# The last chunk of w_down: earlier sums copied into the banks ahead of the products

## The chip, the core and the metric

The kernel runs on one core of a Trainium2 chip. The metric is device time in microseconds (us), the median of several runs. A core has five engines that work through their own instruction queues and wait for each other by semaphores: PE (matrix products into eight PSUM banks of 128 x 512 fp32), ACT and DVE (elementwise work; both reach SBUF and PSUM), POOL and SP (here used to issue DMAs; POOL's can add into their destination, SP's can't).

## The reference

One encoder layer on 512 tokens of width 2048, all in fp32: RMSNorm, one input projection, dilated attention beside gated linear attention, output projection, residual. Then the part that matters here:

```python
h = rmsnorm(x, ffn_norm_w[l])
x = x + (jax.nn.silu(h @ w_gate[l]) * (h @ w_up[l])) @ w_down[l]
return rmsnorm(x, final_norm_w)
```

The hidden width is 5632, so w_down is 5632 x 2048.

## The kernel before

**fp32 from three products.** Every operand is split into a rounded part hi and a rest lo; a product is hi·hi + hi·lo + lo·hi, three matmuls. ACT makes hi by a copy that rounds, DVE makes lo by a subtraction. In `Down.products` the three are L2022 (needs hi), L2023 (needs lo of w_down) and L2024.

**w_down in seven products.** The class `Down` computes most of `g @ w_down` by a Strassen-like scheme with seven products in place of eight, M0 to M6 (`n` in the code, in the order of `ORDER`: 0, 6, 1, 3, 4, 2, 5). The rows of w_down that it covers are cut into four chunks of eight 128-row tiles, the columns into two halves C of 1024. `run` walks through `seq`: chunk, then C, then the seven products k, then two depths d. One entry is a **step** of 12 matmuls. A product is two steps long and fills two banks. A half is 14 steps; the code calls the steps of the last half of the last chunk l = 0 to 13, and those of the half before it are l = -14 to -1.

**A step's own work.** `cast(i+2)` on ACT (L1991) and `sub(i+2)` on DVE (L1999) make hi and lo for the step after next. From the fourth product on the operand is a sum of blocks, made one step earlier by `add(i+3)` on DVE (L1976, L1979). `evac_late` copies the two banks of the product that has just ended to SBUF (ACT, L2062 for n = 4, which changes the sign, L2064 for the others).

**What happens to a product's sum.** Its copy goes to `md` in DRAM: written by SP in the first chunk (L2069), added to what is there by an accumulating DMA from POOL in the others (L2067). After the last chunk each of the 14 sums (two halves of seven) must be read back: `fetch` (L2045, a DMA on POOL's queue, 512 KB). For the half C = 0 this stands at l = 1 to 7, for C = 1 at l = 5 to 13 and after the loop. The very last product (C = 1, n = 5) is not added in DRAM; DVE adds its banks to the fetched sum (L2057).

**Combining.** `combine(C)` turns the seven sums into four outputs in seven entries of two DVE additions each (L2084). `step(C, n)` does the next n entries; for C = 0 they stand at l = 5 to 11, for C = 1 in the first job after `run` (1, 0, 3, 3 entries in its four parts). `seed` (L2101, ACT) copies four results into banks, on which a later job then accumulates.

**What follows.** Four jobs `later_jobs`, one for each 512 columns, add 4 more row tiles of w_down onto the seeded banks; each has four parts of 12 matmuls (L346, L347, L348). Their w_down pieces come through the stream `st`: SP loads 512 KB (L209), ACT rounds a half piece (L237), DVE takes the rest (L218). `g_load` and `g_split` (L1816, L1824 to L1828) do the same for the tiles of g. At the end of a job `residual` (L1847, DVE, four times) adds the banks to x; `seed(c+1)` stands in the job's third part. Then `finish` does the last four row tiles and the final norm.

**What sets the order.** The order in each queue is that of the program text, written out by hand. SBUF buffers come from two pools of slots, first in first out: `s4` (33 slots of 4 KB per partition) and `s2`. An instruction that takes a slot waits for the slot's last user. `load` keeps at most eight raw blocks of w_down at a time.

Of the kernel before, what the change touches and what calls it, by code (L numbers as in the profile page):

```python
# [18 lines left out]
AF = mybir.ActivationFunctionType  # L19
OP = mybir.AluOpType  # L20
# [92 lines left out]
def put(*slots):  # L113
    for s in slots:
        if s.home is not None:
            s.home.free.append(s.i)


def layer(nc, tc, x, attn_norm_w, w_in, rel_table, gw_f, gb_f, gw_b, gb_b, gla_norm_w, w_out,
# [3 lines left out]
    w_gate, w_up, w_down, out = w_gate[0], w_up[0], w_down[0], out[0]  # L123
    pe, act, dve, pool, sp = nc.tensor, nc.scalar, nc.vector, nc.gpsimd, nc.sync
    mm = pe.matmul

    with tc.manual_schedule(), \
# [5 lines left out]
        s2 = Slots(p2, N2, 512, "a")  # L133
        s4 = Slots(p4, N4, 1024, "b")
        ps = Slots(pp, 8, 512, "ps")
# [107 lines left out]
        st = Stream()  # L243
# [44 lines left out]
        class Job:  # L288
# [5 lines left out]
            banks = None  # L294
# [996 lines left out]
        for pr in range(2):  # L1291
            j = job("B", [piece512(w_in, C_GV + pr * 512, k) for k in range(0, KT, 2)], list(range(KT)), acts_h,
                    evac_gv(pr), rate=RATES[0], start=None if pr else gstart, limit=3,
                    before=(lambda i: load_gates() if i == 12 else None) if pr else before_first)
# [144 lines left out]
        j = job_out(0, 0, KT, evac_out(0), rate=RATES[1], start=start_out(0), before=load_first)  # L1439
# [437 lines left out]
        class Down:  # L1877
# [1 line left out]
            ORDER = ((0, 1, "B11"), (6, 2, "T4"), (1, 3, "B21"), (3, None, "T1"), (4, None, "T3"), (2, None, "T2"),  # L1879
                     (5, None, "B22"))  # L1880
            FREES = {0: "B11", 4: "T13", 2: "T24", 5: "F2"}
            FETCH = (0, 1, 2, 4, 3, 6, 5)
            AHEAD = 2

            def __init__(self, chunks):
                self.chunks = chunks
                self.end = len(chunks) - 1
                self.seq = [(ch, C, k, d) for ch, duos in enumerate(chunks) for C in range(2) for k in range(7)
                            for d in range(len(duos))]
                self.todo = deque((ch, C, d, blk) for ch, duos in enumerate(chunks) for C in range(2)  # L1890
                                  for blk in (1, 2, 3, 0) for d in range(len(duos)))
                self.raw, self.src, self.sets = {}, {}, {}
                self.x = {}
                self.making = self.operands()
                self.late = []
                self.m, self.y = {}, {}
                self.ops = {0: self.combine(0), 1: self.combine(1)}

            def load(self):
# [108 lines left out]
            def products(self, i):  # L2008
                ch, C, k, d = self.seq[i]
                n, _, name = self.ORDER[k]  # L2010
                hi, lo = self.sets.pop(i)
                first, last = d == 0, d == len(self.chunks[ch]) - 1
                if first:
                    self.banks = [ps.get() for _ in range(2)]
                q = self.chunks[ch][d]
                for j in range(2):
                    xh, xl = self.x[q + j][name]
                    wh, wl = hi.t[:, j], lo.t[:, j]
                    for h in range(2):
                        o = self.banks[h].t  # L2020
                        t = slice(h * P, (h + 1) * P)
                        mm(o, xh[:, t], wh, start=first and j == 0, stop=False)  # L2022
                        mm(o, xh[:, t], wl, start=False, stop=False)  # L2023
                        mm(o, xl[:, t], wh, start=False, stop=last and j == 1)  # L2024
                put(hi, lo)
                if C == 1 and n in self.FREES:
                    for j in range(2):
                        slots = self.x[q + j]["slots"][self.FREES[n]]
                        state["big"] -= sum(x_.home is s4 for x_ in slots)
                        put(*slots)  # L2030
                        if n == 5:
                            self.x.pop(q + j)
                if last:
                    self.late.append((ch, C, n, self.banks))

            def fetch(self, C, n):

                if len(s4.free) > 8:
                    o = s4.get(F32, [P, 2, 512])
                    m = []  # L2040
                    for i in range(2):
                        v = Slot()
                        v.t, v.f, v.i, v.home = o.t[:, i], o.t[:, i], o.i, None if i else s4
                        m.append(v)
                    pool.dma_start(out=o.t, in_=md[14 * C + 2 * n:14 * C + 2 * n + 2].rearrange("h p c -> p h c"))  # L2045
                else:
                    m = [s2.get() for _ in range(2)]
                    for h in range(2):
                        pool.dma_start(out=m[h].t, in_=md[14 * C + 2 * n + h])
                self.m.setdefault(C, {})[n] = m  # L2050

            def evac(self, ch, C, n, banks):

                for h, bank in enumerate(banks):
                    if ch == self.end and C == 1 and n == 5:
                        m = self.m[C][n][h].t
                        dve.tensor_tensor(m, m, bank.t, op=OP.add)  # L2057
                        put(bank)
                        continue
                    y = s2.get()  # L2060
                    if n == 4:
                        act.activation(y.t, bank.t, AF.Copy, scale=-1.0)  # L2062
                    else:
                        act.copy(y.t, bank.t)  # L2064
                    put(bank)
                    if ch:
                        pool.dma_start(out=md[14 * C + 2 * n + h], in_=y.t, accum_op=OP.add)  # L2067
                    else:
                        sp.dma_start(out=md[14 * C + 2 * n + h], in_=y.t)  # L2069
                    put(y)  # L2070
# [32 lines left out]
                    put(*y[0][c % 2], *y[1][c % 2])  # L2103

            def run(self):
                n_last = len(self.seq) - 7 * len(self.chunks[-1])
                for i, (ch, C, k, d) in enumerate(self.seq):
                    self.load()
                    self.cast(i + self.AHEAD)
                    self.add(i + self.AHEAD + 1)  # L2110
                    self.sub(i + self.AHEAD)
                    self.load()
                    self.evac_late()
                    q = self.chunks[ch][d]
                    while q not in self.x or q + 1 not in self.x:
                        self.make(1)
                    l = i - n_last
                    if l == 13:
                        for t in range(4):
                            self.seed(0, t)  # L2120
                    self.products(i)
                    if i % 14 in (0, 1, 2, 5, 11, 12, 13):
                        self.make(1)
                    run_urgent()
                    if 1 <= l < 8:
                        self.fetch(0, self.FETCH[l - 1])
                    if 5 <= l < 12:
                        self.step(0, 1)
                    if l >= 5 and l % 2:
                        self.fetch(1, self.ORDER[(l - 5) // 2][0])  # L2130
                    if l == 8:
                        self.fetch(1, 5)
                        g_load(LAST // 2 - 2)
                        st.until, st.limit = None, 1
                        st.load()
                    if l == 10:
                        g_split(LAST // 2 - 2)
                        g_load(LAST // 2 - 1)
                        st.limit = 2
                        st.load()  # L2140
                    if l in (11, 12):
                        st.split(later_first + l - 10)
                self.evac_late()
                self.fetch(1, 2)
                st.limit, st.big = 3, tail_first

        def evac_later(c):
# [5 lines left out]
        def before_later(c):  # L2153
            def f(i):
                j = LAST // 2 - 2 + (c + 1)
                if c and i == 0:
                    g_load(j)
                if i == (2 if c else 0) and c < 3:
                    g_split(j)
                if c == 0:  # L2160
                    dn.step(1, (1, 0, 3, 3)[i])
                if i == 1:
                    x1[c] = [s2.get() for _ in range(4)]
                    for t in range(4):
                        sp.dma_start(out=x1[c][t].t, in_=xd[4 * c + t])
                if i == 2 and c < 3:
                    for t in range(4):
                        dn.seed(c + 1, t)
            return f
# [12 lines left out]
        later_first = len(st.halves)  # L2182
# [148 lines left out]
```

## Time and profile before

| | before |
|---|---|
| median of 3 runs | 2158.2 us (2157.49 to 2159.44) |
| profiled execution, own time | 2156.48 us |
| its span | 2154.7 us |
| PE busy | 2129.7 us (99%) |
| DVE busy | 1827.4 us (85%) |
| ACT busy | 1249.3 us (58%) |
| POOL busy | 422.9 us (20%) |
| granted TensorE clock, mean | 0.995 |

The span is what the profile covers, from the first instruction to the end of the last one; the execution's own time is 1.8 us more. Times in rows of the trace count from the start of the span. A row of the timeline has start, duration, engine, line, operation, result and operands, how many instructions are merged, and in brackets the idle time before it and what ended it.

### The profile page before, as it was taken

What the parts mean: (1) busy time and instruction counts of PE and PEld (TensorE: products, weight loads), DVE (VectorE), ACT (ScalarE), POOL (GpSimd) and SP (SyncE); (2) the same over time, 40 slices, a digit from 0 to 9 for tenths busy, and PEclk for the clock granted to TensorE, in tenths of its full rate; (3) what the DMA queues carried; (4) which work ended last, traced back from release to release, by engine and by line L of the source; (5) the groups of instructions that cost most, each with busy time, mean ns of one, the idle gap of its engine ahead of it and who ended that gap; (6) DMA issues with size and microseconds to landing.
All of it is one profiled execution on the core that took longest, in us unless ns stands there. A gap on an engine that the chain in (4) does not pass through costs nothing.

```text
span 2154.7 us, 32578 instructions
## 1 busy us (share of the span) xinstructions
PE 2129.7 (99%) x11410; PEld 1827.7 (85%) x11410; DVE 1827.4 (85%) x3004; ACT 1249.3 (58%) x2251; POOL 422.9 (20%) x571
## 2 busy tenths in 40 slices
PE   9999999999999999999999999999999999999988
PEld 7888888888878889888888888888888888888767
DVE  6699999789878778899898999998989888897775
ACT  8455555478876456455555555555555676675542
POOL 0011222332222110021212121221122210333400
PEclk9999999999999999999999999999999999999999
DMA  6377777877676762577677677776777997999972
GB/s 203 133 183 182 180 179 184 209 212 215 194 231 214 247 241 91 150 182 181 180 179 197 171 184 183 179 193 174 181 189 175 288 277 216 231 207 254 241 276 78
DMA packets 274306, 423.68 MB, mean 197 GB/s; under 512 B 20253, under 2 KB 164877, under 8 KB 274142
## 3 DMA queue, kind: packets, MB, share of 16 engines
q1 hardware_dynamic: 205102, 272.75, 39.6%
q0 software_dynamic: 68720, 148.31, 32.1%
q8 instruction: 90, 1.47, 0.3%
q14 instruction: 74, 0.61, 0.1%
q10 hardware_dynamic: 320, 0.53, 0.1%
HBM read 289.57 MB, written 78.74 MB: 171 GB/s over the span
## 4 chain that ended last, share of the span: by engine, by line
PE 48%; issue 5%; POOL 3%; DMA 2%; DVE 1%; ACT 0%; SPq 0%; POOLq 0%; DVEq 0%; ACTq 0%
PE ps L1603 25%; PE ps L1589 12%; POOL md L2067 2%; PE ps L2024 2%; PE ps L2022 2%; PE ps L2023 2%; DMA b<-in_w_down_dram 1%; PE ps L347 1%; PE ps L348 1%; PE ps L346 1%; DMA b<-md 1%; PE ps L2228 1%; PE ps L2226 1%; PE ps L2227 1%; DMA gd<-b 0%
## 5 line engine op out<-in xcount | busy, mean ns | idle before, releaser
L1506 ACT CAST b<-b 128x1024 fp32r<-128x1024 f32 (+1 forms) x473 | 433.5, 944 | 294.7 <-DVE b L1511 196.6
L1603 PE MATMUL ps<-b,b 128*128 128x512 f32 x1760 | 517.2, 393 | 0.4 <-ACT b L1506 0.2
L1511 DVE TENSOR_TENSOR b<-b,b 128x1024 fp32r<-128x1024 f32 (+1 forms) x473 | 495.7, 1083 | 18.4 <-ACT b L1506 8.5
L1603 PE MATMUL ps<-a,b 128*128 128x512 f32 x1488 | 436.5, 393 | 0.5 <-DVE b L1623 0.4
L1603 PEld LDWEIGHTS ps<-b,b 128*128 128x128 f32 x1760 | 298.1, 188 | 33.2 <-ACT b L1506 0.7
L1589 PEld LDWEIGHTS ps<-b,b 128*128 128x128 f32 x1760 | 289.9, 190 | 42.4
L1589 PE MATMUL ps<-b,b 128*128 128x256 f32 x1760 | 318.0, 280 | 0.0
L1589 PEld LDWEIGHTS ps<-a,b 128*128 128x128 f32 x1488 | 246.6, 189 | 39.1 <-DVE b L1511 0.4
L1603 PEld LDWEIGHTS ps<-a,b 128*128 128x128 f32 x1488 | 248.9, 188 | 25.8 <-ACT b L1506 0.6
L1589 PE MATMUL ps<-a,b 128*128 128x256 f32 x1488 | 267.5, 280 | 0.0
L1999 DVE TENSOR_TENSOR b<-b,b 128x1024 fp32r<-128x1024 f32 x112 | 135.9, 1220 | 36.0 <-ACT b L1991 34.2
L1493 DVE TENSOR_TENSOR b<-b 128x512 f32<-128x512 f32 x212 | 144.8, 683 | 1.8 <-DMA grd<-b 1.0
L1991 ACT CAST b<-b 128x1024 fp32r<-128x1024 f32 x112 | 115.4, 1051 | 38.0 <-DVE b L1979 23.1
L347 PE MATMUL ps<-b,b 128*128 128x512 f32 x324 | 127.8, 394 | 7.6 <-DVE b L218 7.6
L346 PE MATMUL ps<-b,b 128*128 128x512 f32 x324 | 132.2, 408 | 0.3 <-ACT b L460 0.3
L1648 POOL DMA_DIRECT2D b<-a x58 | 50.3, 867 | 413.7 <-ACT b L1506 257.0
L348 PE MATMUL ps<-b,b 128*128 128x512 f32 x324 | 127.8, 394 | 0.2 <-DVE b L464 0.2
L2067 POOL DMA_DIRECT2D md<-a x82 | 72.3, 969 | 213.5 <-ACT a L2064 192.1
L1654 POOL DMA_DIRECT2D b<-a x58 | 50.2, 866 | 283.6 <-DMA b<-a 158.1
L1494 DVE TENSOR_TENSOR b<-b,b 128x256 f32<-128x256 f32 x212 | 90.1, 425 | 7.4
L1495 DVE TENSOR_TENSOR b<-b,b 128x256 f32<-128x256 f32 x212 | 90.2, 425 | 7.3
L346 PE MATMUL ps<-a,b 128*128 128x512 f32 x236 | 94.3, 400 | 0.0
(308 smaller groups left out, 4181.5 us busy)
## 6 DMA issues: line engine op xcount, KB each, us to landing
b<-in_w_gate_dram SPq DMA_DIRECT2D x109, 512.0 KB, 3.9
b<-in_w_in_dram SPq DMA_DIRECT2D x94, 512.0 KB, 3.9
b<-in_w_up_dram SPq DMA_DIRECT2D x88, 512.0 KB, 4.3
b<-in_w_down_dram SPq DMA_DIRECT2D x88, 512.0 KB, 8.0
b<-a POOLq DMA_DIRECT2D x174, 256.0 KB, 4.6
md<-a POOLq DMA_DIRECT2D x82, 256.0 KB, 6.8
b<-in_w_out_dram SPq DMA_DIRECT2D x32, 512.0 KB, 4.5
gd<-b POOLq DMA_DIRECT2D x22, 512.0 KB, 3.9
```

The source lines that it names most:

```text
L346: mm(o, xh.t[:, c], wh.t[:, w], start=first and not on, stop=False, skip_group_check=on)
L347: mm(o, xh.t[:, c], wl.t[:, w], start=False, stop=False, skip_group_check=on)
L348: mm(o, xl.t[:, c], wh.t[:, w], start=False, stop=last, skip_group_check=on)
L1493: dve.tensor_tensor(s_[:, :, 0:2], r[:, :, 1:3], r[:, :, 0:1].to_broadcast(shape), op=OP.add)
L1495: dve.tensor_tensor(s_[:, :, 3], s_[:, :, 2], r[:, :, 3], op=OP.add)
L1506: act.copy(o, src)
L1511: dve.tensor_tensor(o, src, h, op=OP.subtract)
L1589: mm(o, wl, xh, start=False, stop=end, skip_group_check=True)
L1603: mm(o.rearrange("p (s t) -> p s t", s=2), wh, x_, start=first and p == 0, stop=False, skip_group_check=True)
L1991: act.copy(hi.t, self.src[i].t)
L1999: dve.tensor_tensor(lo.t, s.t, hi.f, op=OP.subtract)
L2067: pool.dma_start(out=md[14 * C + 2 * n + h], in_=y.t, accum_op=OP.add)
```

## The change

In the last chunk no sum goes to DRAM any more. Each of the 14 sums of the first three chunks is fetched by SP, in place of POOL, four steps ahead of its product. One step ahead of the product the new `put_back` copies it into the two banks (ACT), and the product's first matmul accumulates onto them in place of starting afresh. When the product has ended, `evac` copies the banks back over the fetched buffers, and that is the full sum; the accumulating DMA is left out, as is the addition on DVE for the last product. The entries of `combine` are spread otherwise: for C = 0 at l = -7, 1, 2, 3, 5, 7, 9; for C = 1 at l = 11 and then 0, 2, 2, 2 in the parts of the first job. The first loads of g and of the stream for the later jobs stand at l = 6 and 9 (before: 8 and 10), the splits at l = 10 and 12 (before: 11 and 12), `g_split` at l = 9 (before: 10).

```diff
                 if first:
-                    self.banks = [ps.get() for _ in range(2)]
+                    self.banks = self.seeded.pop((C, n)) if ch == self.end else [ps.get() for _ in range(2)]
+                new = first and ch < self.end
...
-                        mm(o, xh[:, t], wh, start=first and j == 0, stop=False)
+                        mm(o, xh[:, t], wh, start=new and j == 0, stop=False, skip_group_check=True)
...
             def fetch(self, C, n):
...
-                    pool.dma_start(out=o.t, in_=md[14 * C + 2 * n:14 * C + 2 * n + 2].rearrange("h p c -> p h c"))
+                    sp.dma_start(out=o.t, in_=md[14 * C + 2 * n:14 * C + 2 * n + 2].rearrange("h p c -> p h c"))
...
+            def put_back(self, C, n):
+
+                banks = self.seeded[C, n] = [ps.get() for _ in range(2)]
+                for h, bank in enumerate(banks):
+                    m = self.m[C][n][h].t
+                    if n == 4:
+                        act.activation(bank.t, m, AF.Copy, scale=-1.0)
+                    else:
+                        act.copy(bank.t, m)
+
             def evac(self, ch, C, n, banks):
 
                 for h, bank in enumerate(banks):
-                    if ch == self.end and C == 1 and n == 5:
-                        m = self.m[C][n][h].t
-                        dve.tensor_tensor(m, m, bank.t, op=OP.add)
-                        put(bank)
-                        continue
-                    y = s2.get()
+                    y = self.m[C][n][h] if ch == self.end else s2.get()
...
                     put(bank)
+                    if ch == self.end:
+                        continue
...
             def run(self):
-                n_last = len(self.seq) - 7 * len(self.chunks[-1])
+                n_last = len(self.seq) - 14
                 for i, (ch, C, k, d) in enumerate(self.seq):
+                    l = i - n_last
+                    for s_ in range(2):
+                        p = l + 14 * (1 - s_) + 4
+                        if p % 2 == 0 and 0 <= p < 14:
+                            self.fetch(s_, self.ORDER[p // 2][0])
                     self.load()
                     self.cast(i + self.AHEAD)
                     self.add(i + self.AHEAD + 1)
                     self.sub(i + self.AHEAD)
                     self.load()
                     self.evac_late()
+                    for s_ in range(2):
+                        p = l + 14 * (1 - s_) + 1
+                        if p % 2 == 0 and 0 <= p < 14:
+                            self.put_back(s_, self.ORDER[p // 2][0])
...
-                    if 1 <= l < 8:
-                        self.fetch(0, self.FETCH[l - 1])
-                    if 5 <= l < 12:
+                    if l in (-7, 1, 2, 3, 5, 7, 9):
                         self.step(0, 1)
-                    if l >= 5 and l % 2:
-                        self.fetch(1, self.ORDER[(l - 5) // 2][0])
-                    if l == 8:
-                        self.fetch(1, 5)
+                    if l == 11:
+                        self.step(1, 1)
+                    if l == 6:
                         g_load(LAST // 2 - 2)
                         st.until, st.limit = None, 1
                         st.load()
-                    if l == 10:
+                    if l == 9:
                         g_split(LAST // 2 - 2)
                         g_load(LAST // 2 - 1)
                         st.limit = 2
                         st.load()
-                    if l in (11, 12):
-                        st.split(later_first + l - 10)
+                    if l in (10, 12):
+                        st.split(later_first + (l - 8) // 2)
                 self.evac_late()
-                self.fetch(1, 2)
...
                 if c == 0:
-                    dn.step(1, (1, 0, 3, 3)[i])
+                    dn.step(1, (0, 2, 2, 2)[i])
```

More of the change, by code (lines that the diff above doesn't have):

```diff
@@ L1881, in layer @@
             FREES = {0: "B11", 4: "T13", 2: "T24", 5: "F2"}
-            FETCH = (0, 1, 2, 4, 3, 6, 5)
             AHEAD = 2
@@ L1896, in __init__ @@
                 self.m, self.y = {}, {}
+                self.seeded = {}
                 self.ops = {0: self.combine(0), 1: self.combine(1)}
@@ L2021, in products @@
                         t = slice(h * P, (h + 1) * P)
-                        mm(o, xh[:, t], wh, start=first and j == 0, stop=False)
-                        mm(o, xh[:, t], wl, start=False, stop=False)
-                        mm(o, xl[:, t], wh, start=False, stop=last and j == 1)
+                        mm(o, xh[:, t], wh, start=new and j == 0, stop=False, skip_group_check=True)
+                        mm(o, xh[:, t], wl, start=False, stop=False, skip_group_check=True)
+                        mm(o, xl[:, t], wh, start=False, stop=last and j == 1, skip_group_check=True)
                 put(hi, lo)
@@ L2048, in fetch @@
                     for h in range(2):
-                        pool.dma_start(out=m[h].t, in_=md[14 * C + 2 * n + h])
+                        sp.dma_start(out=m[h].t, in_=md[14 * C + 2 * n + h])
                 self.m.setdefault(C, {})[n] = m
+            def put_back(self, C, n):
[6 more added lines that the diff above has]
+                        act.copy(bank.t, m)
             def evac(self, ch, C, n, banks):
                 for h, bank in enumerate(banks):
-                    if ch == self.end and C == 1 and n == 5:
-                        m = self.m[C][n][h].t
-                        dve.tensor_tensor(m, m, bank.t, op=OP.add)
-                        put(bank)
-                        continue
-                    y = s2.get()
+                    y = self.m[C][n][h] if ch == self.end else s2.get()
                     if n == 4:
@@ L2116, in run @@
                         self.make(1)
-                    l = i - n_last
                     if l == 13:
```

## The prediction

> **What bounds the kernel now.** I read the page first: PE is busy nearly all the time, so the change can only win what PE loses, plus slow matmuls. Then busy time by stretches, cut where the last half, the jobs and the final part begin, to find where PE loses.
>
> ```profile
> PE 2129.7 (99%) x11410; PEld 1827.7 (85%) x11410; DVE 1827.4 (85%) x3004; ACT 1249.3 (58%) x2251; POOL 422.9 (20%) x571
> ...
> 2003.60:2036.30 32.70, 32.70 (x146) 27.04 (x144) 23.43 (x24) 17.24 (x24) 17.87 (x22) 1.00 0.98 264
> 2036.30:2046.90 10.60, 7.22 (x26) 5.53 (x25) 10.04 (x14) 7.99 (x14) 3.73 (x5) 0.84 1.07 312
> 2046.90:2060.50 13.60, 13.60 (x62) 11.21 (x60) 5.05 (x9) 6.31 (x13) 3.72 (x7) 1.00 1.06 353
> 2060.50:2078.10 17.60, 8.65 (x26) 6.15 (x25) 14.03 (x23) 7.63 (x15) 0.00 (x0) 0.71 0.88 320
> 2078.10:2102.50 24.40, 24.40 (x109) 20.19 (x109) 21.79 (x36) 11.02 (x20) 0.00 (x0) 1.00 0.52 183
> ```
>
> The columns are PE, PE's weight loads, DVE, ACT and POOL, the granted clock, DMA share and GB/s. Two stretches lose, and in both the clock is down too. The matmuls on their edges give the sum. First the rate: two pairs of bank copies on ACT that wait for PE, five products apart, give 27.20 / 5 = 5.44 us for 24 matmuls, so 0.2267 each and 2.72 us a step.
>
> ```profile
> 1992.27 1.28 ACT L2062 ACTIVATE a<-ps 128x512 f32<-128x512 f32 x2 [2.23 <-PE ps L2024]
> 1993.44 1.99 ACT L1991 CAST b<-b 128x1024 fp32r<-128x1024 f32 x2
> ...
> 2019.47 1.31 ACT L2064 COPY a<-ps 128x512 f32<-128x512 f32 x2 [2.23 <-PE ps L2024]
> ```
> ```profile
> 2036.27 0.39 PE L2022 MATMUL ps<-b,b 128*128 128x512 f32 x1
> 2040.04 0.79 PE L2023 MATMUL ps<-b,b 128*128 128x512 f32 x1 [3.38 <-DVE b L1999]
> 2046.62 0.39 PE L2024 MATMUL ps<-b,a 128*128 128x512 f32 x1
> ...
> 2060.45 0.39 PE L346 MATMUL ps<-b,b 128*128 128x512 f32 x1
> 2068.43 0.79 PE L347 MATMUL ps<-b,b 128*128 128x512 f32 x1 [7.59 <-DVE b L218]
> 2075.27 0.50 PE L347 MATMUL ps<-b,a 128*128 128x512 f32 x1 [1.36 <-DVE b L218]
> 2077.92 0.39 PE L346 MATMUL ps<-b,b 128*128 128x512 f32 x1
> ```
>
> 2036.27 is the first matmul of step 12, 2046.62 the last of step 13: 23 spacings take 10.35 us in place of 5.21, **loss one 5.1 us**. From 2060.45 (second part of job 1) to 2077.92 there are 24 spacings: 17.47 in place of 5.44, **loss two 12.0 us**. Together 17.1 us, waits and slow matmuls after them. Both wait for a DVE subtraction, so I ask what DVE was waiting for.
>
> ```profile
> 2007.72 1.22 DVE L1976 TENSOR_TENSOR b<-b,b 128x1024 f32<-128x1024 f32 x1
> ...
> 2020.01 1.22 DVE L1999 TENSOR_TENSOR b<-b,b 128x1024 fp32r<-128x1024 f32 x1
> 2021.15 1.28 DVE L2084 TENSOR_TENSOR b<-b,b 128x512 f32<-128x512 f32 x2
> ...
> 2026.22 1.29 DVE L2084 TENSOR_TENSOR b<-b,b 128x512 f32<-128x512 f32 x2 [1.51 <-DMA b<-md]
> ...
> 2036.42 1.29 DVE L2084 TENSOR_TENSOR b<-b,b 128x512 f32<-128x512 f32 x2 [3.16 <-DMA b<-md]
> 2038.77 1.22 DVE L1999 TENSOR_TENSOR b<-b,b 128x1024 fp32r<-128x1024 f32 x1
> ...
> 2064.07 3.70 DVE L2084 TENSOR_TENSOR b<-b,b 128x512 f32<-128x512 f32 x6 [12.12 <-DMA b<-md]
> 2067.69 0.68 DVE L218 TENSOR_TENSOR b<-b,b 128x512 fp32r<-128x512 f32 x1
> ...
> 2071.91 2.71 DVE L1847 SCALAR_TENSOR_TENSOR a<-ps,small,a 128x512 f32<-128x512 f32 x4
> 2074.54 4.29 DVE L218 TENSOR_TENSOR b<-b,b 128x512 fp32r<-128x512 f32 x7
> ```
>
> Three combine entries wait for a reload from md: 1.51, 3.16 and 12.12 us, and the subtractions that PE needs stand behind them. The last reload was itself late, because its read had to wait until the last accumulation had landed:
>
> ```profile
> 2056.82 0.76 POOL L2045 DMA_DIRECT2D b<-md  x1 [5.09 <-DMA md<-a]
> ...
> L2045 POOL DMA_DIRECT2D b<-md x14: 751/1251/1317, 2005.3 to 2056.8; - x14
> ...
> DMA to landing us min/median/max: 6.7/10.6/17.1
> ```
>
> **Part by part.** *The round trip.* After the change no combine entry waits for a DMA at all: its operands are buffers that ACT has just refilled. That removes the three waits. Whether both losses go with them depends on what DVE and ACT still have to do, so I count it.
>
> *DVE in the last half.* An operation on 1024 columns costs 1.14 us (2021.15 - 2020.01), a combine entry 1.21 (2038.77 - 2036.42 - 1.14). DVE first takes up the sums of blocks at 2007.72; with two bank copies now between ACT's casts, 1.1 later, at 2008.8. From there to the end of `add(13)` the new order has 8 additions, 7 subtractions, 5 entries and the 2 operations of `g_split` (0.61 each, 4.29 / 7): 17.1 + 6.0 + 1.2 = 24.3, so 2033.1. `sub(12)` ends at 2034.3, against 2036.27 when PE wants it: **2.0 us in hand**, where it was 3.5 late.
>
> *ACT: the new copies.* 28 copies into banks. The nearest row is the seed copy, SBUF to bank:
>
> ```profile
> 2041.83 2.16 ACT L2101 COPY ps<-b 128x512 f32<-128x512 f32 x4
> 2044.01 1.28 ACT L174 ACT_TABLE_LOAD   x1
> ...
> 2050.00 2.73 ACT L237 CAST b<-b 128x512 fp32r<-128x512 f32 x5
> 2060.02 1.14 ACT L237 CAST b<-b 128x512 fp32r<-128x512 f32 x2 [7.29 <-DMA b<-in_w_down_dram]
> ...
> 2063.85 0.63 ACT L1824 ACTIVATE b<-b 128x512 fp32r<-128x512 f32 x1 [1.85 <-DMA b<-gd]
> ```
>
> 0.54 each, 1.1 a pair; the upper bound is the copy out of a bank, 1.31 / 2. A product's 5.44 us then hold a pair out (1.2), a pair in (1.1), two casts (2.0): 4.3, so ACT stays below PE. But the order matters. The pair in stands behind `cast(2k+1)`, which from the fourth product on waits for DVE's addition, and PE needs it a step earlier than it needed that cast. For the last product: `add(13)` 2033.1, cast 1.0, pair 1.1 gives 2035.2, against 2036.27: **1.0 us in hand**, the thinnest place of the change. I cost it at nothing; if the cover is gone (each us that DVE or the load of g is later), PE waits by as much. ACT's two extra copies out, in place of DVE's L2057, end after that.
>
> *The first job.* Now the entries for C = 1 lie here without their wait, but they are still work. Without loss one, step 13 ends at 2036.27 + 5.44 = 2041.7. ACT copies its banks out (done 2042.4), loads a table (1.28), casts a half piece (0.55): 2044.2. From there DVE does four subtractions (2.4), `g_split` (1.2, and 0.5 until ACT delivers), six entries (7.2), the residual (2.7) and the subtraction that job 1's third part needs (0.6): 2058.8. PE is there at 2041.7 + 6 x 2.72 = 2058.0. **A wait of 0.9 us stays** (lower bound 0.6, as the part's first matmul needs only hi).
>
> How much does such a wait cost in slow matmuls? By the rows, 1.6 us followed the 3.38 us wait, in proportion 0.4 here. [...]
>
> *DMAs.* Removed: 28 additions into md less the 2 that were never made, 256 KB each. Moved from POOL to SP: the 14 reloads. On SP each takes about 0.34 of issue time, against gaps of several us between its issues there. What was queued behind POOL's waits are the four loads of final_norm_w, wanted last of all. In the window from 2036 to 2070 the queues took:
>
> ```profile
> q0 software_dynamic: 2046, 5.74, 56.3%
> q1 hardware_dynamic: 3128, 6.16, 49.6%
> ...
> 2017.20 0.34 SPq L1816 DMA_DIRECT2D b<-gd  x1
> ```
>
> POOL's queue, most of it md traffic, held more than half of the engines' time. That goes from just the stretch in which w_down, x and g arrive late (2060.02, 2063.85). *SP's order.* The reload stands in front of w_down's loads and waits for a slot. By the last row SP issued what stands at the end of step 8 (PE there at 2028.1) 11 us ahead of PE; a reload four steps ahead is thus issued some 15 us or more before its product. In the code fewer slots are free then (about 7 in place of 14), which shortens the lead by some two steps; I take nothing for it.
>
> **The sum.** -17.1 + 0.9 = -16.2. Against the profiled execution's own 2156.5: 2140.3. The median of the runs shown stands 1.7 above that execution, so in medians 2158.2 - 16.2 = **2142.0 us**.
>
> **Rivals.** *A, late arrivals.* The loads of w_down and g land when they do now. For: the waits at 2060.02 and 2063.85. Then ACT splits g until 2065.0 and its seeds for job 2 are done at 2067.1, while PE wants them at 2064.4: 2.7 more, with a slow clock about 4. Or the 1.0 us in hand at step 12 is not there: 2 to 4 us. Together 2145 to 2151. Against: the md traffic is gone from that window.
>
> *B, loss two isn't md's.* The chain of waits runs from 2044.90 to 2070.10 through loads of w_down, not through md. Then only loss one goes: 2153. Against: ACT's five casts at 2050.00 show that the pieces for these parts had been there for long; DVE alone stood in front of them.
>
> *C, slower: the reload becomes the wait.* If SP can't run ahead, a reload is issued when PE is four steps, 10.9 us, before the product. With its landing (10.6 median) and 1.1 for the copies it is 0.8 late; at the longest landing of 17.1 it is 7.3 late. As each is issued by PE's own progress, this adds up over 14 products. The gain is eaten from 17.1 / 14 = 1.2 late, a landing of 11.0; at 12 us it is 2.2 x 14 = 31 late, 2172. For: slots are scarce. Against: the 11 us lead above. [...]
>
> *D, no change.* What is won here is waited for later, for the last pieces of w_down: 2158. Against: from 2078.1 to 2102.5 PE runs without a gap at a DMA share of 0.52, so those pieces have room.
>
> **Chances.** Forecast 0.63, A 0.18, B 0.08, C 0.07, D 0.04. The forecast's own range is 2140.5 to 2145. The range for 8 in 10 goes from 2140 to 2151: the forecast and A. A measurement of this kernel tells about 0.2%, 4 us, from no change; forecast, A and B are faster by that, so 0.89 faster, 0.04 same, 0.07 slower.
>
> **What would show it.** Right: no L2084 waits for a DMA; steps 12 and 13 run without a gap at clock 1.00; DVE's 12.12 us are gone; one wait of about 0.9 us at L347 in job 1's third part; POOL issues nothing after the third chunk but final_norm_w. Wrong: PE waiting for the new bank copies ahead of products (C), waits for w_down or g in ACT's rows that hold up seeds (A), or 7 us and more still lost in job 1 with md gone (B).

## The result, and the profile after

The changed kernel takes 2140.95 us (median of 4 runs, 2140.30 to 2141.89), against 2158.07 before (4 runs). The ratio is 0.992, 95% interval 0.9903 to 0.9937. The profiled execution took 2140.30 with a span of 2138.5, 16.2 us less than the 2154.7 before.

The list of PE's waits from 1900 on was led by 8.9 and 3.4 us before. After, of the whole span, it reads (us in total, times, longest):

```profile
PE ps L1188 <- DVE warm L436: 1.1, 1, 1.1
PE ps L1603 <- DVE b L1623: 0.8, 2, 0.6
PE ps L347 <- DVE b L218: 0.6, 1, 0.6
```

The first two lie in earlier parts of the kernel. Of all that PE waited for in the last chunk and the jobs, 0.6 us are left. Busy time by stretches, cut where the forecast had the parts of the program begin (the second row is steps 12 and 13, the next two are jobs 0 and 1; in this profile each part begins about 0.4 us later):

```profile
2003.60:2036.30 32.70, 32.70 (x146) 27.09 (x145) 30.40 (x35) 25.50 (x39) 2.24 (x4) 1.00 0.43 138
2036.30:2041.70 5.40, 5.40 (x26) 4.46 (x25) 2.40 (x4) 3.70 (x8) 0.00 (x0) 1.00 0.99 360
2041.70:2052.60 10.90, 10.90 (x50) 9.03 (x49) 7.41 (x13) 10.50 (x19) 0.00 (x0) 1.00 1.05 391
2052.60:2063.50 10.90, 10.30 (x46) 8.20 (x45) 10.90 (x19) 8.42 (x16) 0.00 (x0) 1.00 0.58 181
```

In the last half ACT rises from 17.24 to 25.50 us of 32.70 and the DMA share falls from 0.98 to 0.43; the clock is 1.00 throughout. On DVE's timeline the entries (now L2092) stand without a wait for a DMA:

```profile
2032.71 1.22 DVE L1979 TENSOR_TENSOR b<-b,b 128x1024 f32<-128x1024 f32 x1
2033.84 1.22 DVE L1999 TENSOR_TENSOR b<-b,b 128x1024 fp32r<-128x1024 f32 x1
...
2045.19 0.69 DVE L218 TENSOR_TENSOR b<-b,b 128x512 fp32r<-128x512 f32 x1 [6.44 <-ACT b L237]
...
2056.04 2.72 DVE L1847 SCALAR_TENSOR_TENSOR a<-ps,small,a 128x512 f32<-128x512 f32 x4
2058.67 4.30 DVE L218 TENSOR_TENSOR b<-b,b 128x512 fp32r<-128x512 f32 x7
```

The 6.44 us are free time of DVE in step 13 and at the start of job 0; the last row begins with the subtraction for which PE waits 0.6 us. On ACT's timeline one wait is new:

```profile
1970.18 1.11 ACT L2061 COPY ps<-b 128x512 f32<-128x512 f32 x2 [2.50 <-DMA b<-md]
...
2034.91 1.10 ACT L2061 COPY ps<-b 128x512 f32<-128x512 f32 x2
```

The second reload had not landed when ACT came to it; the slowest of the reloads on L2046 took 14.8 us from issue to landing. Its copy ended at 1971.29; PE's first matmul of that product starts at 1971.39. PE did not have to wait, by 0.1 us.

### The profile page after: what moved, and what is told of

It is laid out like the page before. It is cut to its first block, busy times and chain, and to the rows that moved or that the text cites. A ratio compares the mean times of both kernels' runs of the same rounds, so it can differ in the third digit from the quotient of the medians.

```text
span 2138.5 us, 32543 instructions
## 1 busy us (share of the span) xinstructions
PE 2126.0 (99%) x11410; PEld 1825.3 (85%) x11410; DVE 1826.6 (85%) x3002; ACT 1264.8 (59%) x2281; POOL 388.7 (18%) x531
## 4 chain that ended last, share of the span: by engine, by line
PE 56%; DVE 1%; DMA 1%; ACT 1%; issue 0%; SPq 0%; DVEq 0%; ACTq 0%
PE ps L1603 25%; PE ps L1589 13%; PE ps L2024 5%; PE ps L2023 5%; PE ps L2025 5%; PE ps L347 1%; PE ps L348 1%; PE ps L346 1%; PE ps L2240 1%; PE ps L2239 1%; PE ps L2238 1%; DMA a<-xd 0%; DMA gd<-b 0%; ACT b L237 0%; DVE a L1847 0%
## 5 line engine op out<-in xcount | busy, mean ns | idle before, releaser
L1603 PE MATMUL ps<-a,b 128*128 128x512 f32 x1488 | 436.4, 393 | 0.6 <-DVE b L1623 0.6
L347 PE MATMUL ps<-b,b 128*128 128x512 f32 x332 | 129.9, 391 | 0.0
L218 DVE TENSOR_TENSOR b<-b,b 128x512 fp32r<-128x512 f32 x116 | 77.0, 685 | 20.7 <-ACT b L237 20.5
L1629 ACT COPY a<-ps 128x256 f32<-128x256 f32 x58 | 21.6, 372 | 122.0 <-PE ps L1589 121.8
```

The source lines that it names most:

```text
L347: mm(o, xh.t[:, c], wl.t[:, w], start=False, stop=False, skip_group_check=on)
L1603: mm(o.rearrange("p (s t) -> p s t", s=2), wh, x_, start=first and p == 0, stop=False, skip_group_check=True)
```

## The experiments

The theory behind the forecast: PE's losses came from DVE's queue, where the subtractions stood behind combine entries that waited for a reload. Rivals: md's traffic slowed the loads of w_down, x and g; or the new places of entries and loads are what wins; or the reload becomes a wait of its own.

### Only the order on DVE

```diff
 # the kernel before
-                if c == 0:
-                    dn.step(1, (1, 0, 3, 3)[i])
+                if c == 1 and i == 1:
+                    dn.step(1, 7)
```

> The kernel before, with one edit: all seven combine entries of the second half stand in job 1's second part, behind the subtractions for the halves up to there, in place of 1, 0, 3, 3 in job 0. The reloads stay as they are and as late. Theory (the subtractions stood behind entries that waited for md): loss two can no longer begin at 2060 in job 1's second part; the entries wait until about 2064, take 8.5 us, the seeds for job 2 are done near 2075 where PE wants them near 2069, so PE waits about 6 us there plus some slow matmuls: loss two falls from 12 to 6 to 9 us, 2152 to 2155 us in all. Rival (the pieces of w_down, slowed by md's traffic, are late): the wait in job 1 stays where it is, 2158.

Measured: 2145.09 us (before: 2157.08), ratio 0.9941 (0.9926 to 0.9955): 12.0 us less. Nothing of the round trip was changed. PE's waits from 1900 on and DVE's entries:

```profile
PE ps L2023 <- DVE b L1999: 4.0, 1, 4.0
```
```profile
2060.10 2.49 DVE L218 TENSOR_TENSOR b<-b,b 128x512 fp32r<-128x512 f32 x4
2062.50 1.29 DVE L2084 TENSOR_TENSOR b<-b,b 128x512 f32<-128x512 f32 x2
2064.91 7.31 DVE L2084 TENSOR_TENSOR b<-b,b 128x512 f32<-128x512 f32 x12 [1.12 <-DMA b<-md]
```

The reload is as late as before (DVE can go on at 2064.91, before: 2064.07), but nothing that PE needs soon stands behind it. Loss two is gone entirely, loss one stays. I had expected 6 us of it to come back at job 2, but the seeds need only some of the entries each and follow them one by one, so they were done in time. The pieces of w_down still arrive as late as before (ACT waits for them until 2060.75) and cost PE nothing: the rival that the chain of waits suggested falls.

### Only the queue of the reloads

```diff
 # the kernel before, in fetch
-                    pool.dma_start(out=o.t, in_=md[...])
+                    sp.dma_start(out=o.t, in_=md[...])
```

> The kernel before, with the reloads from md on SP in place of POOL, at the same places of the program. Theory (what counts is that the sum goes to DRAM and back just ahead of its use): the reloads still wait for the accumulation that precedes them, and now SP's loads of w_down, x and g stand behind that wait: no gain, 2156 to 2170. Rival (the gain is the faster queue): the reloads land some us earlier and losses one and two shrink, 2145 to 2152.

Measured: 2147.98 us, ratio 0.9954 (0.994 to 0.9969). My theory was wrong here: 9.1 us less where it said no gain, and inside the rival's range. PE's waits are 5.6 us at L347 (two, the longest 3.2) and none at step 12. POOL and SP around the last reload:

```profile
2038.60 1.75 POOL L2067 DMA_DIRECT2D md<-a  x2 [5.50 <-ACT a L2064]
...
2040.80 7.06 SPq L2045 DMA_DIRECT2D b<-md  x2
2047.95 0.94 SPq L209 DMA_DIRECT2D b<-in_w_down_dram  x2
2048.98 1.94 SPq L2165 DMA_DIRECT2D a<-xd  x4
```

In the kernel before POOL's reloads waited for free slots, and accumulations stood behind them. These rows are of the kernel before:

```profile
2021.66 2.78 POOL L2045 DMA_DIRECT2D b<-md  x3
...
2044.26 0.75 POOL L2045 DMA_DIRECT2D b<-md  x1 [6.45 <-PE ps L2023]
2045.00 1.80 POOL L2067 DMA_DIRECT2D md<-a  x2
```

Those last accumulations had their data at 2041.42, when ACT's copy of the banks ended, and were held until 2045.00 by the reload ahead of them, 3.6 us. With the reloads on SP they go out at 2038.60, as ACT delivers their data (which is 2.6 us earlier there, as loss one is gone). So the reloads did not only wait for the accumulations, they also delayed them. Loss one went because the reloads landed sooner: the three that POOL issued from 2021.66 on took 14.7 us or more each, and the entry at 2036.42 waited for the first of them; on SP the longest of the 14 took 12.1 us. Whether the queue itself or what stood in it made the difference, this run doesn't separate. What the theory had right shows too: SP's loads of w_down and x now stand behind the last reload until 2047.95.

### One half alone

Only one value of C is seeded; the other half goes through DRAM as before.

```diff
 # the kernel after
+            NEW = (0,)        # or (1,)
...
-                    self.banks = self.seeded.pop((C, n)) if ch == self.end else [ps.get() for _ in range(2)]
-                new = first and ch < self.end
+                    self.banks = self.seeded.pop((C, n)) if ch == self.end and C in self.NEW else [ps.get() for _ in range(2)]
+                new = first and not (ch == self.end and C in self.NEW)
```

> The kernel after, but only the first half of the columns (C = 0) is seeded; C = 1 is added in DRAM and reloaded by POOL as before, its entries 1, 0, 3, 3 in job 0. Theory (waits for md): loss one (5.1) goes, as its entries are of C = 0; loss two stays nearly whole, since its entry waits for the last reload of C = 1: 10 to 13 us, 2151 to 2154. Rival (traffic): half of md's traffic is gone and half of both losses with it, 2149 with a remainder of loss one visible at step 12.

> The kernel after, but only C = 1 is seeded; C = 0 is added in DRAM and reloaded by POOL at l = 1 to 7 as before, its entries at l = 5 to 11. Theory (waits for md): loss two goes (12 us, with a wait of 1 to 2 us left in job 1). Loss one hangs on the reloads of C = 0, which no accumulations of C = 1 on POOL's queue hold up any more: 0 to 5 us of it stay. 2141 to 2147. Rival (traffic): as for C = 0 alone, about 2149.

Measured: C = 0 alone 2150.64 us, ratio 0.9972 (0.9963 to 0.9982); C = 1 alone 2139.25 us, ratio 0.9916 (0.9901 to 0.9931). The first median lies between the theory's 2151 and the rival's 2149, so the trace has to decide. With C = 0 alone PE has no wait at step 12, where the rival had a remainder of loss one, and DVE stands in front of job 1 as before:

```profile
2056.86 3.70 DVE L2100 TENSOR_TENSOR b<-b,b 128x512 f32<-128x512 f32 x6 [10.87 <-DMA b<-md]
```

With C = 1 alone both losses are gone, and the median lies below the theory's 2141 to 2147; PE's waits from 1900 on are 0.3 and 0.2 us. Seeding the half C = 0, that is half of the change, wins nothing that C = 1 alone doesn't win.

### The places, and the traffic

> The kernel after, but with the combine entries, the first loads of g and of the stream, and the splits at the places that they have in the kernel before (entries at l = 5 to 11 and 1, 0, 3, 3; loads at 8 and 10; splits at 10, 11, 12). Theory (waits for md): the places matter little once no entry waits for md. By DVE's count no wait at step 12, and 2.5 us in place of 0.6 in job 1's third part: 2142 to 2144. Rival (the new places are what wins): losses one and two come back in part, 2148 or more.

> The kernel after, with ten accumulating DMAs of 256 KB from POOL into rows of md that nothing reads any more, five at l = 9 and five at the start of job 0: 2.5 MB, as much as md moved between 2036 and 2070 in the kernel before. No engine waits for them. Theory (the losses were waits of DVE for md's data): the loads of w_down, x and g land some us later, as in the kernel before, and have that to spare: 0 to 3 us slower than the kernel after, 2141 to 2144. Rival (traffic): a large part of loss two comes back, 2147 to 2153.

The edit of the second (the first moves the lines of `run` and `before_later` back):

```diff
 # the kernel after; gT[k] are tiles of g that g_split has just made
+        def add_md(k, row):
+            src = (*gT[k], *gT[k + 1])
+            for i in range(5):
+                pool.dma_start(out=md[row + i], in_=src[i % 4].f, accum_op=OP.add)
```

Measured on one chip with the kernel after, which took 2139.70 (2138.80 to 2140.23):

> The kernel after, unchanged, on the same chip as the next three: 2140 to 2142.

Old places: 2140.66 us, ratio 0.9923 (0.9908 to 0.9938), with 1.5 us of wait at L347 in place of 0.6. Extra traffic: 2140.80 us, ratio 0.9925 (0.9909 to 0.9942), PE's wait 0.6 us as without it. Both are a little faster than the theory's ranges. The traffic slowed the loads almost to what they were before, and cost PE nothing. Landing times of the stream's pieces from 2000 or 2010 on (min/median/max), first after, then with the extra traffic:

```profile
DMA to landing us min/median/max: 3.7/6.7/8.2
```
```profile
DMA to landing us min/median/max: 6.0/8.6/14.6
```

Before it was 6.3/9.6/16.0. Both rivals fall: neither the places nor this traffic carry the gain. The test of the traffic is partial, though: from 2030 to 2070 POOL's queue moved 3.67 MB, against 1.05 in the kernel after and 7.01 in the kernel before. About 1 MB of each of the three figures is final_norm_w, so the ten DMAs put back less (2.6 MB) than md moved there (6.0), not as much as the expectation says. The last kernel of the section "Without the round trip's removal" tests it in full.

### The lead of the reload and of the copy

```diff
 # the kernel after, first kernel: fetch; second kernel: put_back
-                        p = l + 14 * (1 - s_) + 4
+                        p = l + 14 * (1 - s_) + 2
...
-                        p = l + 14 * (1 - s_) + 1
+                        p = l + 14 * (1 - s_)
```

> The kernel after, with each reload two steps ahead of its product in the program, in place of four. Theory (SP runs ahead of PE by the free slots, so that the place in the program is not the time of issue): the first reloads, which share the DMA queues with the last accumulations, land late and PE waits once or twice for their bank copies, 1 to 5 us in all; the later ones land in 3 to 6 us and cost nothing: 2141 to 2146. Rival (the lead is the place in the program, 5.4 us less the copies, so each of 14 products waits): 14 times 1 us or more, 2155 and up.

> The kernel after, with the copies into the banks in the same step as the product in place of one step ahead. ACT then copies them behind the copies out of the product before, for which it waits on PE: the banks are ready about 1.4 to 2 us after PE could have started (the rest of the copies out, then 0.54 or 1.1). 14 products: 20 to 28 us, 2160 to 2169 at full clock. If short idles make the clock swing, the granted clock falls in that stretch and the time is longer still, up to 2200; if each wait is too short for that, the clock stays at 1.00.

Reload two steps ahead: 2140.26 us, ratio 0.9925 (0.991 to 0.994). PE's one new wait and what ACT waited for:

```profile
1967.32 0.50 PE L2023 MATMUL ps<-b,a 128*128 128x512 f32 x1 [1.42 <-ACT ps L2061]
```
```profile
1966.68 1.11 ACT L2061 COPY ps<-b 128x512 f32<-128x512 f32 x2 [4.65 <-DMA b<-md]
```

One product of 14 waits, the first; the longest landing is 16.2 us, the median 6.4. SP's lead, not the place in the program, covers the rest.

Copy not ahead: 2161.02 us, ratio 1.002 (1.0011 to 1.003), slower than before. Each product waits for its bank copies. Most of the last half and the one before it, and one such wait:

```profile
1964.00:2042.00 78.00, 63.63 (x267) 48.79 (x265) 49.91 (x49) 46.52 (x69) 1.86 (x3) 1.00 0.50 163
```
```profile
1991.90 0.39 PE L2025 MATMUL ps<-b,a 128*128 128x512 f32 x1
1993.52 0.50 PE L2023 MATMUL ps<-b,a 128*128 128x512 f32 x1 [1.24 <-ACT ps L2059]
```

From start to start 1.62 us in place of 0.23, so 1.4 a product, 19.5 for 14. With the next matmuls, a little slow as well (0.34, 0.24 and 0.23 apart), a product takes 6.97 us (1993.52 to 2000.49) in place of 5.44: 1.5 each, 21.4 for 14. Against the kernel after of the runs above, on another chip, the difference of the medians is 21.3 us. That is the price of the one step of lead that `put_back` has, and all of the change's gain.

### Without the round trip's removal

> The kernel before with two edits: the reloads on SP in place of POOL, and the seven entries of C = 1 in job 1's second part. No sum is seeded; all still go through DRAM. Theory as it stands after the first runs (the losses are DVE's queue standing behind late reloads, and nothing of the round trip itself): the move to SP takes loss one, the move of the entries takes loss two, 2139 to 2142, as fast as the kernel after. Rival (the round trip costs something that only the seeding removes): 4 us or more are left, 2144 or above, with a wait of PE in its rows.

Both edits of the first two experiments together: 2145.56 us, ratio 0.9949 (0.9936 to 0.9963). Not the sum, and what the rival forecast: above 2144, with a wait of PE. Loss one and loss two are gone as they were, but a new wait of 3.05 us stands in job 1 (and 0.81 at the start of job 2):

```profile
2056.70 2.74 DVE L1847 SCALAR_TENSOR_TENSOR a<-ps,small,a 128x512 f32<-128x512 f32 x4 [3.77 <-DMA a<-xd]
2059.36 2.48 DVE L218 TENSOR_TENSOR b<-b,b 128x512 fp32r<-128x512 f32 x4
```
```profile
2060.09 0.79 PE L347 MATMUL ps<-b,a 128*128 128x512 f32 x1 [3.05 <-DVE b L218]
```

SP's loads of x stand behind the last reload, as in the second experiment, so the residual on DVE waits for x and the subtraction behind it is late. If that reading is right, the late reload must stand in a queue behind which nothing urgent follows:

```diff
 # the kernel before, in fetch, with the entries of C = 1 in job 1's second part
-                    pool.dma_start(out=o.t, in_=md[...])
+                    (pool if C else sp).dma_start(out=o.t, in_=md[...])
```

> The kernel before with the entries of C = 1 in job 1's second part, and with the reloads of C = 0 on SP, those of C = 1 still on POOL. All sums go through DRAM. Theory (what costs is the queue that stands behind a late reload): the last reload now waits on POOL, where only final_norm_w is behind it, and the entries that need it wait on DVE behind all that PE needs; SP's loads of x and w_down stand behind nothing late. Losses one and two both go: 2139 to 2142, as the kernel after. Rival (the round trip costs by itself, by its traffic too): a wait of 2 us or more stays, 2143 or above.

Measured: 2139.54 us, ratio 0.9918 (0.9904 to 0.9932): as fast as the kernel after, with every sum that the kernel before adds in DRAM still added there, and all 14 read back. PE has no wait at all from 1900 on. That settles it against the rival. In the window from 2036 to 2070 the two DMA queues (POOL's and SP's) together were as full as before, 105.2% against 105.9% of the engines' time:

```profile
q0 software_dynamic: 1491, 4.23, 40.5%
q1 hardware_dynamic: 4013, 8.12, 64.7%
```

The stream's pieces landed as late as before, too (a median of 10.0 us in this window in both), and PE did not wait for them: the traffic of md doesn't carry the gain either.

### The wait that was left

```diff
 # the kernel after
+                    if l in (12, 13):
+                        self.step(1, 2)
...
-                    dn.step(1, (0, 2, 2, 2)[i])
+                    dn.step(1, (0, 1, 1, 0)[i])
```

> The kernel after, with four of the combine entries of C = 1 moved from job 0 into l = 12 and 13, where DVE has nothing to do until ACT has copied step 13's banks out (6.4 us in the profile after). By DVE's count the subtraction that job 1's third part needs is then done some 4 us before PE wants it, so the wait of 0.6 us there goes: 0.6 to 1.0 us faster than the kernel after, within what a comparison of medians can tell, so the trace decides. If something else held up that subtraction (the residual waits for x, or the pieces of w_down), the wait stays.

Measured: 2138.79 us (2137.28 to 2140.02), the kernel after beside it 2139.70. In the trace the 0.6 us at L347 are gone and PE has no wait from 1900 on. The residual now starts in job 0's last part (PE is there from 2049.50 to 2052.22), in place of 2056.04:

```profile
2050.45 2.72 DVE L1847 SCALAR_TENSOR_TENSOR a<-ps,small,a 128x512 f32<-128x512 f32 x4
```

The trace shows that the wait is gone; the runs overlap, so that the kernel is faster is not shown by their times.

## Why the prediction was right, and where it wasn't

**The sum.** Forecast -17.1 + 0.9 = -16.2 and 2142.0 us; the profiled spans differ by 16.2, the medians by 17.1. Both losses are gone. Ahead of the last half PE runs 0.46 us later than before (copies out of the banks at 1992.73 in place of 1992.27), for no cause that I looked for.

**The counts for DVE and ACT.** `add(13)` was to end at 2033.1 and ended at 2033.93; the last copy into banks at 2035.2, ended at 2036.01. PE was later too (its step 12 began at 2036.67), so of the 1.0 us in hand about 0.7 were there. The subtraction in job 1 was to be done at 2058.8 and was at 2059.35; its wait, 0.9 in the forecast, is 0.60 of idle time, and 0.98 from start to start in place of 0.23, so 0.75 lost. With the old places the same count had said 2.5 us, and 1.5 was measured: right in sign, about 1 us too high.

**Rival B** rested on the chain of waits, which led through loads of w_down; the experiment on DVE's order rules it out. **Rival A** had no part: with the loads slowed down again almost to where they were, PE's wait is the same. So the DMA relief that I named beside it is real (the pieces land in 6.7 us in place of 9.6, by the median) and worth nothing measurable. **Rival C** has the right mechanism for the copies, as the kernel without their lead shows, but not for the reloads. A landing near the one that I took for its worst case did come: 14.8 us, at the second product, hidden by 0.1 us. For scarce slots I had taken nothing, and the third chunk's accumulations, which moved at the same time (from 1955 to 1975 POOL's queue took 54.1% of the DMA engines' time, SP's 54.3%), I had not counted. Which of the two made it late is not shown; that it cost nothing was luck, by 0.1 us.

**The step that failed** stands under *DMAs*: "What was queued behind POOL's waits are the four loads of final_norm_w". In the kernel before the last accumulations stood there too, and were held up by the reloads ahead of them. That, and reloads that landed sooner (in 12.1 us at most, in place of 17.1), made the move to SP worth 9.1 us by itself, where I had costed it at SP's issue time alone. The forecast's sum doesn't depend on it, since the change removes those accumulations anyway. But the forecast gave the gain to the removal of the round trip, and that was not needed for it: with the sums still going through DRAM, two moves in the queues won as much (2139.54 us).

**The slow matmuls.** The forecast's sum takes nothing for slow matmuls after its wait of 0.9 us. No run had shown that; the proportion to loss one would have added 0.4. After the 0.60 us that came, the matmuls start 0.34, 0.23 and 0.23 us apart (half speed would be 0.45); waits of 0.81, 1.24, 1.36, 1.41 and 1.42 us in other runs, listed in the last section, were followed by the same. After 3.05 us (the kernel with both moves) seven spacings of 0.42 to 0.59 followed. The short idles of the kernel without the copies' lead, 14 of 1.2 us (17.1 in all), did not bring the clock down: it is 1.00 from 1964 to 2062.

What stays open: how much of the last reload's lateness in the kernel before came from POOL's order and how much from its slots, and why the reloads land sooner from SP; the runs move these together.

## What to carry to other kernels

Before removing a round trip through DRAM, look at which in-order queue stands behind it. Here PE's 17 us were lost in DVE's queue, and moving seven combine entries won 12 of them; with the late reload on a queue that had nothing urgent behind it, the whole gain came with the round trip still there. A wait moved to another queue is paid by what follows there: the two single moves, 12.0 and 9.1 us, gave 11.5 together. A chain that ends in a load tells what landed last, not what PE stood behind.

## What the runs showed of the hardware

With no wait, matmuls of 128x512 start 0.227 us apart (the kernel before, 24 in 5.44 us). After PE's waits of 0.60 us (the kernel after), 0.81 (both moves), 1.24 (copy not ahead), 1.36 (the kernel before), 1.41 (C = 0 alone) and 1.42 (reload two steps ahead) the first spacing is 0.33 to 0.34 and the next ones 0.22 to 0.24. After 3.05 us (both moves) and 3.38 (the kernel before) seven spacings of 0.41 to 0.59 follow, after 6.34 (C = 0 alone) and 7.59 (the kernel before) eleven of 0.42 to 0.60. After 4.02 us (only the order on DVE) the first five are 0.23 to 0.34, and only then come eight of 0.37 to 0.43. The granted clock of the stretches with the long waits was 0.86 (3.05 us, 2052 to 2064), 0.84 (3.38), 0.86 (4.02, 2036 to 2048), 0.68 (6.34, 2056 to 2066) and 0.71 (7.59); of those with 0.60, 0.81 and 1.24 us it was 1.00.

Four copies by ACT of 128x512 fp32 into banks, one after the other, took 2.16 us (the kernel before, 2041.83), 0.54 each; a pair took 1.11 (the kernel after, 2000.28). A pair of them beside two casts and a pair of copies out left ACT waiting 1.23 to 1.24 us of a product's 5.44 for PE (the kernel after, 1998.16 to 2019.92).
